# Context norms folded on GpSimd, and two one-vector modulation banks summed on VectorE

## The chip, the cores and the metric

The kernel runs on one core of one Trainium2 chip. What is measured is the device time of one execution, in microseconds (us); several executions are timed, and one more is recorded by the hardware profiler. The engines are named as the profile names them: PE is TensorE (PEld its weight loads), DVE is VectorE, ACT is ScalarE, POOL is GpSimd, SP is the queue that issues nearly all loads. Each engine works through its own instructions in order.

## What is computed

Two transformer blocks in float32 on 256 tokens of width 1024 (`xT` holds them as 128 partitions x 8 chunks x 256 tokens). The first block is attention and a mixture of 32 experts; the second has two layers with a second token stream, the context, that is modulated, mixed and normed like the tokens in its first layer. Cut to what matters here:

```python
# first block: w_ada is 1024 x 6144
mod = silu(c) @ w_ada + b_ada
shift1, scale1, gate1, shift2, scale2, gate2 = split(mod, 6)
h = rms_norm(x, norm1_g) * (1 + scale1) + shift1
x = x + gate1 * (attention(h) @ w_out)
h2 = rms_norm(x, norm2_g) * (1 + scale2) + shift2
x = x + gate2 * moe_ffn(h2)
# second block, layer 0, the context (256 tokens); modc from ada_w and c_ctx
hc = rms_norm(xc, mix_pre_g) * (1 + scc1) + shc1
y = silu(layer_norm(depthwise_conv31(glu(hc @ w_in)), conv_norm_g, conv_norm_b))   # one of three branches
xc = xc + gc1 * rms_norm(merge_of_branches @ w_out, mix_post_g)
hc2 = rms_norm(xc, ffn_pre_g) * (1 + scc2) + shc2
xc = xc + gc2 * rms_norm(square(relu(hc2 @ w_ff1)) @ w_ff2, ffn_post_g)
# then two layers of the second block on x, with keys and values of the context
```

## The kernel before

**Matrix products.** Each weight block of 1024x512 is loaded, split into a high part (ACT, `whi`, L342) and a low part (DVE, `wlo`, L343), and multiplied with activations that are split in the same way: three matmuls for each product, 96 of them for a block (`lin_steps`, L365).

**Two streams.** The main stream is the first block: `front` (attention up to the residual, L687), `route`, `moe`. Beside it goes the *side* stream, `ctx_pass`: the context through the first layer of the second block. It is emitted in steps between steps of the main stream, while `self.side` is true; its tiles end in s (`whis`, `sqs`) and its PSUM tiles are named `side`. The main stream has the higher priority. A scheduler puts the instructions of both streams in one order per engine by its own estimate of times, and the engines then keep this order. When both are done, the *tail* (`self.tail`) runs the two layers of the second block.

**Modulation banks.** A third of a modulation (2048 of 6144 columns) is a *bank*. The side stream computes six of them: "00", "a1", "a2", then "01", "02", "10". The banks a1 and a2 are the second and third of the first block's `w_ada` and serve a single vector, `s1`; the others serve two vectors. `ada_pieces` (L409) loads a bank in eight rows of 128x2048 (1 MB each), into slots of tiles that the side stream does not yet use (`hhi`, `phi`, `hlo`, `plo`), and works off each row with four matmuls that have the 32 padded vectors as weights and stream 512 columns (L438). At the end ACT copies the sum (L443), four transposes bring it to columns (L446), and DVE adds the bias (L451). The front needs a1 for the gate of its residual and a2 for the norm behind it.

**Norms.** `norm_sums` (L245) squares the 8 chunks in four pieces of 128x512, in turn on ACT (L252) and DVE (L254). `stats_add` (L200) adds the squares over the partitions with one matmul of 128x1 for each chunk and half of the tokens, 16 for a norm. `rstd_from` (L163 to L173) makes the reciprocal root with nine small DVE operations (`rs_vs`, `rs_rs`), `bcast_tok` (L179) brings it to all partitions with two transposes. The side stream has five such norms: of the context itself, of the convolution branch, of the mixer's residual, the one ahead of the feed-forward part, and of the last residual.

**The convolution's norm** (`conv_norm`, L1612) has two forms. In the tail, POOL adds the two halves of the chunks (L1617) and folds the sum to one chunk, one matmul against `ones` sums up and spreads it (L1620), and four DVE operations subtract the mean (L1622). On the side, 16 matmuls sum up (L1629), DVE makes the mean (L1632), two transposes spread it (L179) and eight DVE operations subtract it (L1635). The tail's norms use `folded_stats` (L261): the squares are added on POOL (L272) and folded there to one chunk (`fold`, L192), so that `stats_add` works on that chunk alone.

Of the kernel before, what the change touches and what calls it, by code (L numbers as in the profile page):

```python
# [15 lines left out]
OP = mybir.AluOpType  # L16
# [4 lines left out]
P = 128  # L21
D = 1024
KC = 8
GW = 128
T = 256
# [73 lines left out]
class Builder:  # L99
# [158 lines left out]
    def norm_stats(self, xT):  # L258
        return self.stats_end(self.norm_sums(xT), 1.0 / D)
# [149 lines left out]
    def ada_pieces(self, w, b, sT, badd, mod, nv, slots=(), spool=None):  # L409

        nc = self.nc
        acc = []
# [40 lines left out]
        return [lambda k=k: rows(k) for k in range(KC)] + [end]  # L453

# [966 lines left out]
    def ctx_pass(self, L, cx):  # L1421

        nc, a = self.nc, self.a
        w = lambda c: self.wblk("w_in_2", 0, c)
# [3 lines left out]
        ada = {"a": lambda b: self.ada_bank(a["w_ada"][0], b, self.s1, self.colA[:, 16:64], self.mod1, 1, slots),  # L1428
               "0": lambda b: [f() for f in self.layer_ada(0, L, b, slots)],
               "1": lambda b: [f() for f in self.layer_ada(1, self.L1, b, slots)]}  # L1430
        slots = ["hhi", "phi", "hlo", "plo"]
# [9 lines left out]
        slots = ["raws", "phi", "plo"]  # L1441
# [170 lines left out]
    def conv_norm(self, L, yc, chi, clo, pool):  # L1612
        nc = self.nc
        self.pop_conv(1000)
        if self.tail:
            b = self.t(pool, [P, KC, T], tag="qn")[:, 0:4, :]
            nc.gpsimd.tensor_add(b, yc[:, 0:4, :], yc[:, 4:8, :])  # L1617
            self.fold(b)
            mb = self.ps("tr")[:, :T]
            nc.tensor.matmul(mb, self.ones, b[:, 0, :], start=True, stop=True)  # L1620
            for c in range(0, KC, 2):
                nc.vector.scalar_tensor_tensor(yc[:, c:c + 2, :], mb.unsqueeze(1).to_broadcast([P, 2, T]), -1.0 / D,  # L1622
                                               yc[:, c:c + 2, :], op0=OP.mult, op1=OP.add)
            bc = self.folded_stats(yc, self.t(pool, [P, KC, T], tag="qn")[:, 0:4, :])
        else:
            s = self.ps("tr")
            for c in range(KC):
                for t in range(2):
                    nc.tensor.matmul(s[:, t:t + 1], yc[:, c, t * P:(t + 1) * P], self.ones[:, 0:1],  # L1629
                                     start=(c == 0 and t == 0), stop=(c == KC - 1), skip_group_check=True)  # L1630
            mu = self.st([P, 2], tag="mu")
            nc.vector.tensor_scalar(mu, s[:, 0:2], 1.0 / D, None, op0=OP.mult)  # L1632
            mb = self.bcast_tok([mu[:, 0:1], mu[:, 1:2]])
            for c in range(KC):
                nc.vector.tensor_sub(yc[:, c, :], yc[:, c, :], mb)  # L1635
            bc = self.norm_stats(yc)
# [244 lines left out]
```

## Time and profile before

| | us |
|---|---|
| time, median of 3 runs (lowest to highest) | 2755.56 (2747.72 to 2760.62) |
| the profiled execution | 2754.71 |
| its span | 2752.8 |
| stage: first bank of `w_ada` and first norm | 0 to some 40 |
| stage: attention and w_out of the first block (`front`) | to 262 |
| stage: `route` | to some 320 |
| stage: experts, with the context beside them to some 1276 | to some 1590 |
| stage: tail, two layers | to 2753 |

The banks a1 and a2 lie between 96 and 174 us, the context's norms at 174 to 190, 720 to 754, 887 to 910 and 1256 to 1268 us. Busy time of PE is modelled from the starts of its matmuls, and a matmul of float32 leaves two or more records: eight records of L200 are four matmuls. PEclk in the profile is the clock that PE was granted, as a share of 2.4 GHz; 0.50 is the lower level of 1.2 GHz.

### The profile page before, as it was taken

The page shows a single profiled execution, that of the slowest core. Times are in us where ns is not written, and L with a number is a line of the kernel's source. Part 1 is how long each engine was busy: PE and PEld are TensorE (multiplying, and loading weights), DVE is VectorE, ACT ScalarE, POOL GpSimd, SP SyncE. Part 2 cuts the span into 40 slices and gives each one's busy share as a digit, 9 for nine tenths or more (in the row PEclk, how much of TensorE's full clock was granted, in tenths as well). Part 3 has the DMA queues.
Part 4 walks back from the last instruction along what each step waited for, and adds up shares of the span by engine and source line. Part 5 has one row for each costly group of instructions (what it writes and reads, how often), then busy time and mean ns, then how long its engine had stood idle before and what let it go on. Part 6 is the DMA issues. An engine that isn't in the chain of part 4 may idle for free. (4 is left out here: it accounts for less than half of the span.)

```text
span 2752.8 us, 49781 instructions
## 1 busy us (share of the span) xinstructions
PE 2592.5 (94%) x20358; PEld 2047.0 (74%) x20359; DVE 1626.1 (59%) x3090; ACT 1157.5 (42%) x1987; POOL 322.2 (12%) x334
## 2 busy tenths in 40 slices
PE   7999999999899999999889978899999998999998
PEld 5657877678567777875333477899789987899998
DVE  3465543778554524443121279988546789996655
ACT  2333343333243323431111156765445566656543
POOL 0000000000000000000000025442001055350000
PEclk9989899999999999999999989999999999999999
DMA  9758599989999999999999934326854443344442
GB/s 398 300 226 296 203 401 417 364 347 405 378 357 386 390 361 361 409 419 363 392 392 421 415 129 168 125 105 238 289 203 184 158 180 123 131 146 184 154 184 85
DMA packets 119370, 769.80 MB, mean 280 GB/s; under 512 B 11632, under 2 KB 12016, under 8 KB 52832
## 3 DMA queue, kind: packets, MB, share of 16 engines
q1 hardware_dynamic: 117744, 759.15, 70.6%
q0 software_dynamic: 1392, 7.41, 0.7%
q8 instruction: 162, 2.65, 0.4%
q14 instruction: 72, 0.59, 0.1%
HBM read 762.84 MB, written 3.67 MB: 278 GB/s over the span
## 5 line engine op out<-in xcount | busy, mean ns | idle before, releaser
L343 DVE TENSOR_TENSOR wlo<-raw,whi 128x1024 fp32r<-128x1024 f32 (+1 forms) x288 | 337.6, 1175 | 162.2 <-ACT whi L342 156.6
L365 PE MATMUL lin<-hhi,wlo 128*128 128x256 f32 x1440 | 399.3, 283 | 21.6 <-DVE wlo L343 21.6
L365 PE MATMUL lin<-hhi,whi 128*128 128x256 f32 x1440 | 400.5, 282 | 2.2 <-ACT hhi L284 2.2
L365 PE MATMUL lin<-hlo,whi 128*128 128x256 f32 x1440 | 401.4, 281 | 0.1
L342 ACT ACTIVATE whi<-raw 128x1024 fp32r<-128x1024 f32 (+1 forms) x288 | 276.9, 963 | 257.9 <-PE lin L365 189.3
L981 PE MATMUL mlin<-raw,hG 128*32 128x256 f32 (+2 forms) x2920 | 341.3, 456 | 17.5 <-DMA raw<-in_w_gate_up_dram 17.5
L365 PEld LDWEIGHTS lin<-hhi,wlo 128*128 128x128 f32 x1440 | 269.5, 190 | 37.5 <-DVE wlo L343 33.2
L1585 POOL TENSOR_TENSOR yc<-yc,ctmp 128x256 f32<-128x256 f32 x240 | 252.4, 1075 | 300.6 <-ACT ctmp L1584 300.1
L343 DVE TENSOR_TENSOR wlos<-raws,whis 128x512 fp32r<-128x512 f32 x246 | 166.2, 687 | 196.3 <-ACT whis L342 189.4
L365 PEld LDWEIGHTS lin<-hhi,whi 128*128 128x128 f32 x1440 | 271.0, 189 | 5.8 <-ACT hhi L284 3.7
L365 PEld LDWEIGHTS lin<-hlo,whi 128*128 128x128 f32 x1440 | 272.2, 189 | 3.7 <-issue 2.3
L981 PEld LDWEIGHTS mlin<-raw,hG 128*32 128x32 f32 (+2 forms) x2920 | 129.9, 121 | 178.6 <-issue 110.0
L342 ACT ACTIVATE whis<-raws 128x512 fp32r<-128x512 f32 x246 | 148.9, 627 | 225.6 <-PE side L365 186.2
L365 PE MATMUL side<-hhi,whis 128*128 128x256 f32 x720 | 203.0, 288 | 0.1
L365 PE MATMUL side<-hlo,whis 128*128 128x256 f32 x720 | 199.7, 282 | 0.0
L365 PE MATMUL side<-hhi,wlos 128*128 128x256 f32 x720 | 193.1, 284 | 0.7 <-DVE wlos L343 0.5
L343 DVE TENSOR_TENSOR wlo<-raws,whi 128x1024 fp32r<-128x1024 f32 x108 | 139.0, 1287 | 74.4 <-ACT whi L342 73.8
L1587 DVE SCALAR_TENSOR_TENSOR yc<-gl,cw,yc 128x256 f32<-128x256 f32 x240 | 167.8, 734 | 0.1
L342 ACT ACTIVATE whi<-raws 128x1024 fp32r<-128x1024 f32 x108 | 114.4, 1059 | 118.8 <-PE lin L365 103.8
L1006 PE MATMUL main<-raw,aT 128*32 128x256 f32 (+2 forms) x1408 | 162.6, 453 | 1.1 <-DMA raw<-in_w_down_dram 1.0
L365 PEld LDWEIGHTS side<-hhi,whis 128*128 128x128 f32 x720 | 136.7, 190 | 16.5 <-issue 11.2
L365 PE MATMUL lin<-ahi,whi 128*128 128x256 f32 x528 | 145.7, 279 | 0.0
(603 smaller groups left out, 5737.4 us busy)
## 6 DMA issues: line engine op xcount, KB each, us to landing
raw<-in_w_gate_up_dram SPq DMA_DIRECT2D x120, 2048.0 KB, 11.5
raw<-in_w_down_dram SPq DMA_DIRECT2D x55, 2048.0 KB, 11.1
raw<-in_w_in_dram SPq DMA_DIRECT2D x60, 1024.0 KB, 7.1
raws<-in_w_in_dram SPq DMA_DIRECT2D x95, 512.0 KB, 6.8
raws<-in_w_ff_dram SPq DMA_DIRECT2D x88, 512.0 KB, 8.1
raw<-in_w_ff_dram SPq DMA_DIRECT2D x44, 1024.0 KB, 7.0
phi<-in_ada_w_dram SPq DMA_DIRECT2D x10, 1024.0 KB, 7.4
plo<-in_ada_w_dram SPq DMA_DIRECT2D x10, 1024.0 KB, 7.1
```

The lines of the kernel that those rows point to most:

```text
L342: x = nc.scalar.activation(flat(hi), flat(rows[i]), AF.Copy)
L343: y = nc.vector.tensor_sub(flat(lo), flat(rows[i]), flat(hi).bitcast(F32))
L365: x = nc.tensor.matmul(*args, skip_group_check=True, **kw)
L981: nc.tensor.matmul(d, hT(k), gu[k][c0 // D][:, c0 % D:c0 % D + W], start=False, stop=(k == KC - 1), skip_group_check=True)
L1006: nc.tensor.matmul(pys[h][g * C:(g + 1) * C, :W], st, dn[m][:, c0:c0 + W], start=(m == 0), stop=(m == KC - 1), skip_group_check=True)
L1585: nc.gpsimd.tensor_add(d, d, m)
L1587: self.paced(1, nc.vector.scalar_tensor_tensor(d, x, wcol, d, op0=OP.mult, op1=OP.add))
```

## The change

`norm_stats` on the side goes to `folded_stats`: ACT squares four chunks in one operation of 128x1024 and two more in one of 128x512, DVE squares the last two, POOL adds them up in two operations and folds 512 and 256 columns, and two matmuls of 128x1 remain of the 16. `conv_norm` takes the tail's form on the side too. The banks a1 and a2 go through the new `ada_sums`: DVE multiplies each half of a row, 128x1024, by the vector's entry of each partition and adds it to a sum in the tile `plo` (two operations without a second tensor, L466 of the changed kernel, and 14 with one, L468, for a bank); 16 matmuls of 128x1 with the sum as weights and `ones` as the streamed column (L471) add it over the partitions straight into columns, and DVE adds the bias (L473). The rows have three slots there and not four.

```diff
@@ -256,6 +256,8 @@
         return st
 
     def norm_stats(self, xT):
+        if self.side:
+            return self.folded_stats(xT, self.t(self.cx, [P, 4, T], tag="kv"))
         return self.stats_end(self.norm_sums(xT), 1.0 / D)
 
     def folded_stats(self, xT, b):
@@ -451,6 +453,24 @@
                 nc.vector.tensor_add(dst, pv[:, :, :, v], bb)
 
         return [lambda k=k: rows(k) for k in range(KC)] + [end]
+
+    def ada_sums(self, w, b, scol, badd, mod, slots, spool, acc):
+
+        nc = self.nc
+        for k in range(KC):
+            r = self.t(spool, [P, 2048], tag=slots[k % len(slots)])
+            self.behind_first(nc.sync.dma_start(r, w[k * P:(k + 1) * P, b * 2048:(b + 1) * 2048]))
+            for h in range(2):
+                x, d = r[:, h * D:(h + 1) * D], acc[:, h * D:(h + 1) * D]
+                if k == 0:
+                    nc.vector.tensor_scalar(d, x, scol[:, k:k + 1], None, op0=OP.mult)
+                else:
+                    nc.vector.scalar_tensor_tensor(d, x, scol[:, k:k + 1], d, op0=OP.mult, op1=OP.add)
+        p = self.ps("mm")
+        for j in range(16):
+            nc.tensor.matmul(p[:, j:j + 1], acc[:, j * P:(j + 1) * P], self.ones[:, 0:1], start=True, stop=True,
+                             skip_group_check=True)
+        nc.vector.tensor_add(mod[:, b * 16:(b + 1) * 16], p[:, 0:16], badd[:, b * 16:(b + 1) * 16])
 
     def ada_bank(self, *args):
         for f in self.ada_pieces(*args):
@@ -1425,7 +1445,9 @@
         v = 1
         xc = self.t(cx, [P, KC, T], tag="m8")
         self.behind_first(nc.sync.dma_start(xc, a["ctxT"]))
-        ada = {"a": lambda b: self.ada_bank(a["w_ada"][0], b, self.s1, self.colA[:, 16:64], self.mod1, 1, slots),
+        ada = {"a": lambda b: self.ada_sums(a["w_ada"][0], b, self.s1[:, :, 0], self.colA[:, 16:64],
+                                            self.mod1[:, 0, :], ["hhi", "phi", "hlo"], cx,
+                                            self.t(cx, [P, 2048], tag="plo")),
                "0": lambda b: [f() for f in self.layer_ada(0, L, b, slots)],
                "1": lambda b: [f() for f in self.layer_ada(1, self.L1, b, slots)]}
         slots = ["hhi", "phi", "hlo", "plo"]
@@ -1612,28 +1634,16 @@
     def conv_norm(self, L, yc, chi, clo, pool):
         nc = self.nc
         self.pop_conv(1000)
-        if self.tail:
-            b = self.t(pool, [P, KC, T], tag="qn")[:, 0:4, :]
-            nc.gpsimd.tensor_add(b, yc[:, 0:4, :], yc[:, 4:8, :])
-            self.fold(b)
-            mb = self.ps("tr")[:, :T]
-            nc.tensor.matmul(mb, self.ones, b[:, 0, :], start=True, stop=True)
-            for c in range(0, KC, 2):
-                nc.vector.scalar_tensor_tensor(yc[:, c:c + 2, :], mb.unsqueeze(1).to_broadcast([P, 2, T]), -1.0 / D,
-                                               yc[:, c:c + 2, :], op0=OP.mult, op1=OP.add)
-            bc = self.folded_stats(yc, self.t(pool, [P, KC, T], tag="qn")[:, 0:4, :])
-        else:
-            s = self.ps("tr")
-            for c in range(KC):
-                for t in range(2):
-                    nc.tensor.matmul(s[:, t:t + 1], yc[:, c, t * P:(t + 1) * P], self.ones[:, 0:1],
-                                     start=(c == 0 and t == 0), stop=(c == KC - 1), skip_group_check=True)
-            mu = self.st([P, 2], tag="mu")
-            nc.vector.tensor_scalar(mu, s[:, 0:2], 1.0 / D, None, op0=OP.mult)
-            mb = self.bcast_tok([mu[:, 0:1], mu[:, 1:2]])
-            for c in range(KC):
-                nc.vector.tensor_sub(yc[:, c, :], yc[:, c, :], mb)
-            bc = self.norm_stats(yc)
+        four = lambda: self.t(pool, [P, KC, T], tag="qn")[:, 0:4, :] if self.tail else self.t(pool, [P, 4, T], tag="kv")
+        b = four()
+        nc.gpsimd.tensor_add(b, yc[:, 0:4, :], yc[:, 4:8, :])
+        self.fold(b)
+        mb = self.ps("tr")[:, :T]
+        nc.tensor.matmul(mb, self.ones, b[:, 0, :], start=True, stop=True)
+        for c in range(0, KC, 2):
+            nc.vector.scalar_tensor_tensor(yc[:, c:c + 2, :], mb.unsqueeze(1).to_broadcast([P, 2, T]), -1.0 / D,
+                                           yc[:, c:c + 2, :], op0=OP.mult, op1=OP.add)
+        bc = self.folded_stats(yc, four())
         hb = self.st([P, KC], tag="hb")
         nc.vector.tensor_scalar(hb, L["cbn"], 0.5, None, op0=OP.mult)
         for k in range(KC):
```

From `ada_sums` on the line numbers of the changed kernel are 20 higher than before (2 higher between `norm_stats` and there). The order of the program shows the following.

DVE behind the end of the first context bank, before (`modL` is that bank's modulation; `se`, `srd` and `smx` belong to the attention's softmax, `wlo` to a projection's weights):

```order
L451 TENSOR_TENSOR modL_16_101<-side_327,vec_66 128x4x4 x2
L581 SCALAR_TENSOR_TENSOR se_1195,sden_1204<-se_1195,tab_1190 128x128
L461 SCALAR_TENSOR_TENSOR La_71_334<-modL_16_101,vec_66 128x8
L581 SCALAR_TENSOR_TENSOR se_1195,sden_1213<-se_1195,tab_1190 128x256
L461 SCALAR_TENSOR_TENSOR La_72_336<-modL_16_101,vec_66 128x8
L584 RECIPROCAL srd_1207<-sden_1204 128x1
L584 RECIPROCAL srd_1216<-sden_1213 128x1
L617 TENSOR_SCALAR se_1195<-se_1195,srd_1207 128x128
L617 TENSOR_SCALAR se_1195<-se_1195,srd_1216 128x256
L343 TENSOR_TENSOR wlo_1472<-raw_1434,whi_1471 128x512
```

The same place after (`plo` holds the sum of bank a1, `hhi`, `phi` and `hlo` its rows; `sqs` are squares of the context's first norm):

```order
L466 TENSOR_SCALAR plo_338<-hhi_339,s_6_78 128x1024 x2
L345 TENSOR_TENSOR wlo_1448<-raw_1410,whi_1447 128x512
L468 SCALAR_TENSOR_TENSOR plo_338<-phi_343,s_6_78,plo_338 128x1024 x2
L345 TENSOR_TENSOR wlo_1464<-raw_1410,whi_1463 128x512
L271 TENSOR_TENSOR sqs_634<-m_59_274 128x512
L588 SCALAR_TENSOR_TENSOR se_1202<-tab_1166,main_1203 128x384
L468 SCALAR_TENSOR_TENSOR plo_338<-hlo_347,s_6_78,plo_338 128x1024
L345 TENSOR_TENSOR wlo_1480<-raw_1410,whi_1479 128x512
L468 SCALAR_TENSOR_TENSOR plo_338<-hlo_347,s_6_78,plo_338 128x1024
L345 TENSOR_TENSOR wlo_1496<-raw_1410,whi_1495 128x512
```

Sums have come between the weight splits and the softmax; 30 of the 32 stand ahead of the fourth and last `rs_v` (L163, 128x16) of the front's per-head norms, and two right behind it.

PE at the norm of the mixer's residual, before (`raw` are experts' weights, `hG` their tokens, `side_9385` the sums of squares, `side_9422` the spread result):

```order
L981 MATMUL mlin_9110<-raw_9104,hG_8599 32x256 x4
L981 MATMUL mlin_9111<-raw_9104,hG_8599 32x256 x4
L200 MATMUL side_9385<-ones_72,sqs_9398 128x1 x4
L200 MATMUL side_9385<-ones_72,sqs_9404 128x1 x4
L179 MATMUL side_9422<-cst_68,rs_rs_9412 128x128 x2
L981 MATMUL mlin_9110<-raw_1679_9106,hG_8599 32x256 x4
```

and after (`kv` is the folded sum):

```order
L1001 MATMUL mlin_9054<-raw_9050,hG_8543 32x256 x4
L1001 MATMUL mlin_9055<-raw_9050,hG_8543 32x256 x4
L200 MATMUL side_9339<-ones_72,kv_9329 128x1 x2
L179 MATMUL side_9354<-cst_68,rs_rs_9344 128x128 x2
L1001 MATMUL mlin_9054<-raw_1675_9052,hG_8543 32x256 x4
```

Two matmuls with the folded sum stand where the last eight of the 16 were; the others stood among matmuls ahead of this piece, and the next norm's first squares no longer follow right behind. The transposes again stand directly after them. At the next norm, 15 rows further on, the pair stands in the same way, with a row of expert matmuls on either side.

In the order of SP the loads of both streams stand as before, but for a few places. The instructions of the tail stand in the same order on all engines.

## Rows read from the trace of the kernel before

**Rows 1.** The page: busy time of each engine, then slices (tenths, 68.8 us each).

```profile
PE 2592.5 (94%) x20358; PEld 2047.0 (74%) x20359; DVE 1626.1 (59%) x3090; ACT 1157.5 (42%) x1987; POOL 322.2 (12%) x334
...
PE   7999999999899999999889978899999998999998
...
DMA  9758599989999999999999934326854443344442
```

**Rows 2.** Busy time by engine in three stretches of the front.

```profile
core 0: us, PE busy (x) PEld busy (x) DVE busy (x) ACT busy (x) POOL busy (x), PEclk, DMA share, GB/s
96.30:152.80 56.50, 56.50 (x415) 39.74 (x414) 29.11 (x90) 20.68 (x39) 0.00 (x0) 1.00 0.75 287
152.80:200.00 47.20, 44.39 (x228) 24.99 (x227) 28.51 (x103) 16.63 (x35) 0.56 (x1) 0.82 0.42 159
200.00:262.10 62.10, 59.49 (x422) 37.05 (x425) 34.60 (x128) 25.82 (x69) 0.28 (x3) 0.95 0.92 342
```

**Rows 3.** The same view, columns as above, windows of the MoE stretch.

```profile
720.00:740.00 20.00, 18.29 (x150) 13.32 (x152) 7.62 (x22) 4.53 (x10) 0.43 (x1) 0.82 0.76 299
880.00:920.00 40.00, 35.88 (x342) 25.73 (x341) 22.63 (x64) 9.97 (x21) 0.40 (x1) 0.83 0.93 355
1240.00:1280.00 40.00, 39.13 (x284) 25.11 (x283) 21.07 (x51) 8.06 (x15) 0.94 (x2) 0.96 0.86 321
340.00:1580.00 1240.00, 1178.29 (x9409) 796.39 (x9409) 552.25 (x1173) 369.12 (x700) 14.70 (x33) 0.98 0.97 388
```

**Rows 4.** Timeline of PE, 53 to 55 us (start, duration, then line and operation).

```profile
53.57 1.07 PE L438 MATMUL side<-hlo,s 128*32 128x512 f32 x8
54.45 1.04 PE L438 MATMUL side<-plo,s 128*32 128x512 f32 x8
```

**Rows 5.** Timeline of PE, 173 to 190 us.

```profile
172.88 0.60 PE L446 MATMUL side<-cst,sqs 128*128 128x128 f32 x4
174.26 1.05 PE L200 MATMUL side<-ones,sqs 128*128 128x1 f32 x8 [0.78 <-ACT sqs L252]
...
184.45 1.87 PE L200 MATMUL side<-ones,sqs 128*128 128x1 f32 x8
```

**Rows 6.** The page: costliest groups; busy us, mean ns, then idle before.

```profile
L343 DVE TENSOR_TENSOR wlo<-raw,whi 128x1024 fp32r<-128x1024 f32 (+1 forms) x288 | 337.6, 1175 | 162.2 <-ACT whi L342 156.6
...
L343 DVE TENSOR_TENSOR wlos<-raws,whis 128x512 fp32r<-128x512 f32 x246 | 166.2, 687 | 196.3 <-ACT whis L342 189.4
```

**Rows 7.** Instructions of L438, 95.5 to 153 us (min/median/max ns, first, last start).

```profile
L438 PE MATMUL side<-phi,s x24: 592/605/617, 95.8 to 140.7; 128*32 128x512 f32 x24
```

**Rows 8.** Timeline of DVE, 884 to 916 us.

```profile
887.84 1.29 DVE L343 TENSOR_TENSOR wlos<-raws,whis 128x512 fp32r<-128x512 f32 x2 [4.22 <-ACT whis L342]
```

**Rows 9.** Timeline of PE, 718 to 756 us.

```profile
720.21 1.95 PE L1629 MATMUL side<-ones,y 128*128 128x1 f32 x16 [0.63 <-DVE y L1587]
...
754.12 0.28 PE L365 MATMUL side<-hhi,whis 128*128 128x256 f32 x1
754.23 0.28 PE L365 MATMUL side<-hlo,whis 128*128 128x256 f32 x1
```

**Rows 10.** Groups of GpSimd in the tail; columns as in rows 6.

```profile
L192 POOL TENSOR_TENSOR qn<-qn 128x512 f32<-128x512 f32 x4 | 7.8, 1942 | 0.3
L272 POOL TENSOR_TENSOR qn<-qn,sq 128x512 f32<-128x512 f32 x4 | 7.3, 1853 | 17.3 <-DVE sq L269 9.0 <-ACT sq L271 8.3
...
L192 POOL TENSOR_TENSOR qn<-qn 128x256 f32<-128x256 f32 x4 | 6.0, 1489 | 0.3
...
L192 POOL TENSOR_TENSOR sq<-sq 128x256 f32<-128x256 f32 x4 | 3.0, 739 | 0.3
```

**Rows 11.** Timeline of PE, 884 to 916 us.

```profile
887.90 1.05 PE L200 MATMUL side<-ones,sqs 128*128 128x1 f32 x8
889.79 1.05 PE L200 MATMUL side<-ones,sqs 128*128 128x1 f32 x8 [0.84 <-DVE sqs L254]
892.76 0.41 PE L179 MATMUL side<-cst,rs_rs 128*128 128x128 f32 x2 [1.92 <-DVE rs_rs L173]
```

## The prediction

> **What bounds the kernel now.** I began with the page's busy shares and slices [rows 1]: TensorE (PE) is busy 94% of the span and its row reads 8 or 9 nearly everywhere, so work taken off PE could show. The slices also show the DMA row at 9 (once 8) from the sixth to the 23rd slice, where PE is at 7 to 9 too; two resources are nearly full there, and only one of them is relieved. So the limits have to be read stage by stage, and the tail after 1593 us, which the change leaves alone (the program order of its instructions is the same), drops out of the sum.
>
> In the front I read the busy time of each engine over three stretches [rows 2]. They are cut where DVE does something whose place can be found again in the changed program: the end of the first context bank at 96.3 us (`modL`, L451), the fourth and last `rs_v` of the front's per-head norms at 152.8, and the end of the front at 262.1 (the residual, L687). In the first stretch PE is busy for all 56.5 us at full clock and DVE for 29.1: PE is the bound. In the other two PE is idle for 2.8 and 2.6 us, and the granted clock of the middle one is 0.82, so the half level (1.2 of 2.4 GHz) is taken for part of it.
>
> In the MoE stretch the same view, over 340 to 1580 us, gives a DMA share of 0.97, at 388 GB/s, beside 1178 us of PE [rows 3]. DMA is the limit there, except where it pauses: 720 to 740 (0.76), 880 to 920 (0.93) and 1240 to 1280 (0.86). These are the places of the context stream's norms. The idle share of these windows is 4.8, 2.8 and 5.6 us: 13.2 us, and no relief of PE in the MoE stretch can be worth more than that.
>
> **The banks.** A row of a bank is four 32x512 matmuls, eight records, and the next row starts 0.88 us later [rows 4]. Eight rows and the four L446 transposes (0.60 us [rows 5]) are 7.6 us a bank, 15.3 for the two. In their place come 16 matmuls of 128x1 per bank; four such (eight records) take 1.05 us [rows 5], so 4 us a bank. PE gains 7 us.
>
> DVE pays. 32 operations of 128x1024 come in, and the page has a 128x1024 fp32 tensor operation at 1175 ns [rows 6]; at that price they are 37.6 us (the four without a second tensor may be cheaper, which I leave out). By the program order 30 of them stand between the `modL` and the fourth `rs_v`, that is in the first stretch. Its DVE work becomes 29.1 + 30 x 1.175 = 64.4 us, with a square of the context norm (0.7) about 65, against a stretch of 56.5. PE's own need falls there: 12 bank rows go (four slots with 24 records each, one shown in [rows 7], 96 records) at 0.88, 10.6 us, and 0.6 for L446, and 4 come, so about 49. So DVE takes over as the bound, and the stretch is at least 65 long. It waited for PE and ACT for 27 us before; now sums stand in most of these gaps, but in a fixed order, so I add 0.5 to the 8.5: **+9 us**. The ends are +6 and +20: operations of DVE in a row overlap by some 0.08 us (two of 128x512, 687 ns each [rows 6], take 1.29 us together [rows 8]), which makes 1.095 of 1.175; and 11 us of the old waits may remain.
>
> From 152.8 to 262.1 PE gains: the last four rows (3.5), L446 (0.6), and the first context norm. Its 16 matmuls against `ones` ran at half clock for part, the first four in 1.05 us and the last four in 1.87 [rows 5]; the four groups make 6.1 and two waits before them 1.6, of which a pair of matmuls (0.5) stays: 7.2. Against that stand the second bank's 16 small matmuls (4.0). And by the program order 50 projection matmuls of the context now stand in the w_out part, ahead of the end of the front, where none stood before; at 0.115 us from start to start [rows 9] that is 5.8. 11.3 - 4.0 - 5.8 is **-1.5 us**. The 50 matmuls are about half a 512-column block of weights (1 MB of 2 MB), which the MoE stretch then need not load: at 388 GB/s **-2.5 us**.
>
> **The folded norms.** Each loses 14 of 16 small matmuls, 3.5 us of PE at 0.25, and gets a chain on GpSimd (POOL): two adds of 128x512, a fold of 512 and one of 256. POOL adds nothing up for the context before, so the price is read from the tail: 1853, 1942 and 1489 ns, a chain of 7.1 us. Another 128x256 fold of the tail takes 739 ns [rows 10]; with all four at half their price it is 3.6. DVE splits weights beside it here, but does less than in the tail, so I take 5.5, and 1 us for the squares ahead.
>
> *Conv norm* (720 us). The 16 matmuls for the mean (eight of them are the 1.95 us of [rows 9]) become one of 128x256, and the 16 for the squares become two: about 7 us off PE. The POOL add of 128x1024 (some 3 us, by 1.9 for 512 [rows 10]) and two chains take their place, but one DVE pass in four operations replaces eight, and the squares no longer stand behind expert matmuls on PE. I take the whole pause, **-4.8 us**.
>
> *Residual norm and second norm* (886 to 910 us). Before, PE worked off the first norm's last squares from 887.9, waited 0.84 for a square and 1.92 for the `rs_rs` chain of nine small operations, and had the transposes out at 893.2 [rows 11]. In the changed order the two matmuls and the two transposes stand directly one behind the other, and the expert matmuls behind both. PE waits for the POOL chain (6.5 us, less some 2 of expert work in front) and then again for 1.9. So what is saved (3.5 each) is spent: **0**, from -2.8 (the pause of this window goes) to +6 (two waits of 3 us added).
>
> *Last residual norm* (1256 us). Again two matmuls for 16, 3.5 us, in windows with 5.6 us of pause. Nothing of the context stands behind it: **-3.5 us**, from -5.6 to 0.
>
> The Trainium skill ("SBUF — State Buffer", Who interferes with whom) says that a DVE operation with two SBUF inputs and a GpSimd operation that reads SBUF hold a shared port pair exclusively, and the second one is fully blocked; this speaks against putting adds on POOL next to weight splits. The two prices of the 128x256 fold in the tail, 1489 and 739 ns [rows 10], agree with it, but no row before shows such an add beside a weight split of the context. By the rule in full the chains are at the dear end, 1.6 us each, and five of them and the mean's adds move the sum from 2751 to some 2758; by the cheap end it would be some 2745.
>
> **The sum.** The profiled execution took 2754.7 us (span 2752.8), 0.9 below the median of the three runs, 2755.6. 2754.7 + 9 - 1.5 - 2.5 - 4.8 + 0 - 3.5 = **2751 us**, 0.15% below. The measurement cannot tell less than about 0.5% (13.8 us) from no change, so this is "no change". Its own range is 2742 to 2768: the upper end has the first stretch at +20 and a gain of 5 less at the norms.
>
> **Rivals.**
> *All of PE's relief counts.* The sums fit into DVE's 27 idle microseconds of the first stretch without delaying what PE waits for, and DMA closes all its pauses: 7 + 7.2 in the front, 13 in the MoE stretch, 27 us, **2728**. For it: PE is at 100% in the first stretch, DVE at half. Against it: 65 us of DVE work in 56.5. A milder form, the first stretch at +2 with the pauses closed, gives about 2738. Chance of either 0.28.
>
> *DVE becomes the bound and the loss stays*, the rival on the slower side. The mechanism is the DVE queue from 96 to 153 us: a weight split or a softmax step stands behind two sums (2.35 us), PE waits for it, and the last query and key projection arrives late; what follows is a chain through attention and w_out that nothing shortens. The price: the stretch at 75 to 82 us instead of 56.5, +18 to +25, with gains of 4 left elsewhere: **2769 to 2776**. If PE's waits bring the half level of the clock into this stretch, as the middle one shows it, it is dearer: by the 1.87 to 1.05 of [rows 5], a fifth of PE's 49 us at that level adds 8. It decides against my forecast from a distance of about 75 us between `modL` and the fourth `rs_v`. Chance 0.22.
>
> *The POOL chain stalls PE at each of the norms* and the pauses stay: front +5, nothing else, **2760**. Here the change does not do what it is said to do, and it lies within no change.
>
> **How the numbers follow.** Faster by over 0.5% (below 2741.8): 0.28, from the first rival. Within 0.5%: 0.50, of which about 0.15 is the POOL rival. Slower (above 2769.3): 0.22. The range is 2730 to 2774: it leaves out the lower tail of the first rival (a tenth) and the upper end of the second (a tenth).
>
> **What would show it.** In the profile after: DVE busy near 65 us between `modL` and the fourth `rs_v`, and that distance 65 to 70 us with PE idle in it by 10 or more (the first rival: below 60; the second: above 75). The residual L687 at 268 to 272 instead of 262. The two context norms near 890 us with waits of PE side transposes and `ones` matmuls of 3 to 7 us; the DMA share at 720 to 740 above 0.9, and at 1240 to 1280 above 0.9. The tail must have its length of before, 1160 us; if that moves by more than 3 us, the change touches something that I have not seen. Wrong would be above all a cheaper or dearer accumulate operation than 1.175 us, and waits on the three row slots (one less than before) in the front, which would hold the sums back although DVE is free.

## The result

The changed kernel takes 2769.6 us in the median (2763.4 to 2778.8), the kernel before 2753.5 in the runs beside it: a ratio of 1.0066, 95% interval 1.0054 to 1.0079. It is 0.66% slower, some 18 us, where I had forecast no change at 2751 us. The profiled execution of the changed kernel took 2773.35 us with a span of 2771.6, 18.8 more than before.

The first line of the page after answers to [rows 1]: PE lost 17 us of work, DVE and POOL gained 35 each, and the span still grew.

```profile
PE 2575.5 (93%) x20114; PEld 2044.9 (74%) x20115; DVE 1661.5 (60%) x3112; ACT 1159.0 (42%) x1985; POOL 357.3 (13%) x357
```

Busy time by engine after, in windows cut where [rows 2] were cut (`modL`, the fourth `rs_v`, the end of the front, here the start of its last residual operations, 1.1 us ahead of the cut in [rows 2]), then to the first expert matmul, to the tail's first `rs_v`, and the tail (columns: length; busy time of PE, PEld, DVE, ACT, POOL; granted clock; DMA share; GB/s):

```profile
98.10:172.30 74.20, 58.11 (x371) 50.85 (x372) 66.56 (x121) 23.38 (x43) 6.92 (x4) 0.86 0.70 269
172.30:288.20 115.90, 103.55 (x648) 66.38 (x648) 62.74 (x230) 39.40 (x97) 0.79 (x3) 0.81 0.65 233
...
288.20:346.90 58.70, 57.14 (x389) 53.58 (x390) 34.81 (x139) 21.20 (x41) 5.59 (x11) 0.80 0.48 165
346.90:1618.90 1272.00, 1188.76 (x9468) 798.41 (x9467) 564.18 (x1194) 381.68 (x715) 40.40 (x57) 0.97 0.95 383
1618.90:2771.60 1152.70, 1088.67 (x8738) 1020.92 (x8738) 893.13 (x1309) 665.02 (x1037) 300.87 (x269) 0.98 0.45 164
```

The same of before, for the four windows that [rows 2] do not have:

```profile
152.80:261.00 108.20, 102.78 (x640) 61.46 (x640) 62.00 (x228) 41.92 (x101) 0.79 (x3) 0.89 0.70 262
...
261.00:325.90 64.90, 64.26 (x448) 58.67 (x447) 36.00 (x136) 22.91 (x45) 5.20 (x11) 0.82 0.37 131
325.90:1600.30 1274.40, 1202.55 (x9615) 813.78 (x9614) 569.28 (x1216) 379.95 (x717) 16.48 (x38) 0.98 0.96 385
1600.30:2752.80 1152.50, 1088.28 (x8738) 1020.38 (x8738) 890.36 (x1309) 665.41 (x1037) 296.97 (x269) 0.99 0.45 164
```

By stage: 1.8 us ahead of `modL`, +17.7 to the fourth `rs_v`, +7.7 to the end of the front, -6.2 in the route, -2.4 in the MoE stretch, +0.2 in the tail. By the lengths of the stages the loss arises in the front, and nearly a third of it comes back later. The loads tell it a little differently. These are the windows from the start to the first expert matmul, before and then after:

```profile
0.00:325.90 325.90, 301.64 (x2007) 212.83 (x2009) 166.44 (x569) 112.17 (x234) 8.73 (x27) 0.92 0.72 278
```

```profile
0.00:346.90 346.90, 298.10 (x1916) 225.56 (x1920) 204.16 (x611) 112.33 (x233) 16.04 (x31) 0.86 0.71 269
```

The experts start 21 us later, with 93.3 MB moved instead of 90.6. At the 388 GB/s of [rows 3] I estimate these 2.7 MB at 7 us, but the MoE stretch is only 2.4 us shorter: part of the loss arises there too.

**The first stretch** is DVE's. It is busy for 66.6 of 74.2 us (29.1 of 56.5 before), PE for 58. In DVE's timeline one sees the sums in a row with the weight splits:

```profile
98.92 1.41 DVE L466 TENSOR_SCALAR plo<-hhi,s 128x1024 f32<-128x1024 f32 x2
...
100.85 3.48 DVE L468 SCALAR_TENSOR_TENSOR plo<-phi,s,plo 128x1024 f32<-128x1024 f32 x2
...
105.92 2.06 DVE L468 SCALAR_TENSOR_TENSOR plo<-hlo,s,plo 128x1024 f32<-128x1024 f32 x1
107.90 1.74 DVE L345 TENSOR_TENSOR wlo<-raw,whi 128x512 fp32r<-128x512 f32 x1
...
112.97 2.47 DVE L468 SCALAR_TENSOR_TENSOR plo<-hhi,s,plo 128x1024 f32<-128x1024 f32 x2
...
172.32 0.17 DVE L163 TENSOR_SCALAR rs_v<-main 128x16 f32<-128x16 f32 x1 [0.50 <-PE main L557]
```

Two sums take 2.47 us, and the 3.48, 2.06 and 1.74 stand where POOL folds the first context norm. DVE's largest waits in this stretch, with what ended them (us, times, longest), are most of the other 7.6 us:

```profile
DVE y L568 <- PE main L565: 2.6, 1, 2.6
DVE wlo L345 <- ACT whi L344: 2.6, 4, 1.1
DVE se L588 <- PE main L586: 1.1, 1, 1.1
```

PE, which did not stand still here before, waits for 16.1 us:

```profile
PE main L611 <- DVE srd L604: 9.4, 1, 9.4
PE mlin L367 <- DVE wlo L345: 4.3, 3, 3.1
PE mlin L367 <- DVE y L552: 2.4, 1, 2.4
```

The longest wait ends at 166.86 us, when the reciprocal of a softmax (`srd`) is there. In the 9.4 us before that, DVE ran four sums between the steps of this softmax; the last two and the reciprocal are

```profile
162.68 2.47 DVE L468 SCALAR_TENSOR_TENSOR plo<-phi,s,plo 128x1024 f32<-128x1024 f32 x2
...
166.02 0.16 DVE L604 RECIPROCAL srd<-sden 128x1 f32<-128x1 f32 x1
```

The granted clock of this stretch is 0.86, where it was 1.00.

**Behind it** PE waits for rows of the next banks that come late, twice for more than a microsecond (6.4 us of such waits in this window, 1.6 in the same one before):

```profile
221.65 1.94 PE L440 MATMUL side<-phi,s 128*32 128x512 f32 x8 [3.61 <-DMA phi<-in_ada_w_dram]
225.10 1.93 PE L440 MATMUL side<-plo,s 128*32 128x512 f32 x8 [1.51 <-DMA plo<-in_ada_w_dram]
```

The eight records of a row take 1.9 us there, at a granted clock of 0.52 from 220 to 230 us, against 1.07 in [rows 4], where the clock from 50 to 60 us was 1.00.

**In the MoE stretch** the pauses that [rows 3] show did not close (windows moved with the norms; there 0.76, 0.93 and 0.86):

```profile
740.00:760.00 20.00, 18.84 (x136) 10.46 (x136) 8.32 (x19) 4.43 (x9) 7.30 (x7) 0.85 0.76 298
900.00:940.00 40.00, 27.49 (x241) 17.38 (x241) 21.55 (x60) 11.39 (x24) 9.84 (x9) 0.70 0.79 308
1260.00:1300.00 40.00, 34.01 (x216) 18.88 (x216) 18.53 (x45) 6.58 (x12) 5.49 (x6) 0.83 0.83 319
```

The middle one is worse by 0.14. PE's timeline answers to [rows 11]: where a square cost it 0.84, the folded sum costs 5.31, and the chain behind it 1.92 as before.

```profile
909.30 1.01 PE L200 MATMUL side<-ones,kv 128*128 128x1 f32 x4 [5.31 <-POOL kv L192]
...
912.23 0.66 PE L179 MATMUL side<-cst,rs_rs 128*128 128x128 f32 x2 [1.92 <-DVE rs_rs L173]
```

### The profile page after: what moved, and what is told of

Same layout as the page of the kernel before. It is cut to its first block, busy times and chain, and to the rows that moved or that the text cites. A ratio compares the mean times of both kernels' runs of the same rounds, so it can differ in the third digit from the quotient of the medians.

```text
span 2771.6 us, 49339 instructions
## 1 busy us (share of the span) xinstructions
PE 2575.5 (93%) x20114; PEld 2044.9 (74%) x20115; DVE 1661.5 (60%) x3112; ACT 1159.0 (42%) x1985; POOL 357.3 (13%) x357
```

## The experiments

My theory was that DVE's queue in the first stretch makes the loss; the rivals were the folds on POOL, and later the row slots. Each kernel ran in five rounds beside the kernel before (E4 in three). "Idle" is the time that DMA did nothing from the start to the tail's first `rs_v`, summed over windows of 10 us as (1 - DMA share) x length (a share above 1 counts as 1), in the one profiled execution. All kernels move the same 580 MB by then, so this is bookkeeping of where the time went, not a cause. The tail has its old length after the change, but over the experiments it is 1149 to 1164 us long for the same work, and a profiled execution lies up to 10 us from the median of its kernel, so a few us between two profiles show nothing. The ratios come from all executions; the difference of two ratios in the table is uncertain by some 6 to 10 us.

| kernel | banks on DVE | row slots | context norms | ratio (95%) | us by it | idle |
|---|---|---|---|---|---|---|
| before | none | 4 | matmuls | 1 | 0 | 156 |
| the change | a1, a2 | 3 | POOL | 1.0066 (1.0054 to 1.0079) | +18 | 179 |
| E1 | a1, a2 | 3 | matmuls | 1.0066 (1.0043 to 1.0090) | +18 | 167 |
| E2 | none | 4 | POOL | 1.0042 (1.0021 to 1.0063) | +12 | 163 |
| E3 | a1 | 3 | POOL | 0.9967 (0.9951 to 0.9984) | -9 | 139 |
| E4 | a1, a2, half | 3 | POOL | 1.0008 (0.9991 to 1.0026) | +2 | 153 |
| E5 | a1 | 3 | matmuls | 1.0010 (0.9993 to 1.0028) | +3 | 153 |
| E6 | none | 4 | POOL, conv only | 1.0037 (1.0021 to 1.0053) | +10 | 159 |
| E7 | none | 4 | DVE | 0.9993 (0.9977 to 1.0009) | -2 | 151 |
| E8 | a1 | 3 | DVE | 0.9987 (0.9970 to 1.0004) | -4 | 144 |
| E9 | a2 | 3 | POOL | 1.0019 (1.0000 to 1.0038) | +5 | 155 |
| E10 | a1, a2 | 4 | POOL | 0.9998 (0.9977 to 1.0019) | -1 | 153 |
| E11 | none | 4 | POOL, longer | 1.0075 (1.0047 to 1.0102) | +21 | 174 |
| E12 | a1, a2 | 3 | DVE | 1.0049 (1.0028 to 1.0070) | +13 | 164 |
| E13 | a1, a2 | 4 | matmuls | 1.0060 (1.0037 to 1.0083) | +17 | 170 |
| E14 | a1, a2 | 4 | DVE | 0.9970 (0.9952 to 0.9987) | -8 | 146 |
| E15 | none | 3 | matmuls | 1.0039 (1.0021 to 1.0057) | +11 | 167 |
| E16 | a1 | 4 | POOL | 0.9971 (0.9955 to 0.9987) | -8 | 137 |
| E17 | a1, a2 | 4 | first on POOL | 1.0014 (1.0000 to 1.0028) | +4 | 160 |
| E18 | a1 | 4 | DVE | 0.9998 (0.9981 to 1.0016) | -1 | 148 |

### The parts alone

**E1** undoes the norms, **E2** the banks:

```diff
     def norm_stats(self, xT):
-        if self.side:
-            return self.folded_stats(xT, self.t(self.cx, [P, 4, T], tag="kv"))
...
-        ada = {"a": lambda b: self.ada_sums(
+        ada = {"a": lambda b: self.ada_bank(
```

> Only the banks a1 and a2 are summed on DVE; all norms of the context are as before. Theory (DVE queue): the 32 sums of 1.27 us fill DVE between modL and the fourth rs_v, that stretch is 72 to 76 us long and not 56.5, the front ends 24 to 30 us later than before, and the time is 18 to 26 us above before, more than the whole change (+16), since the norms' gain is missing. Rival (POOL folds): the loss comes from the folds on GpSimd, which wait for DVE and hold PE; then this kernel is within 5 us of before.

> Only the norms of the context are folded on GpSimd and its convolution norm takes the tail's form; the banks a1 and a2 go through PE as before. Theory (DVE queue): the front is as before or up to 5 us shorter (first context norm), the MoE stretch gains 2 to 5 us, the time is 2 to 9 us below before. Rival (POOL folds): 10 to 20 us above before, with waits of PE side L200 and L179 of several us at 890 to 910.

E1 went as the theory had it in the stretch (74.1 us) and in the time. Its front ended 18 us later, not 24 to 30, and its profiled execution, the fastest of its six, only 8.6 us later than that of before: as in the changed kernel, part of the front's delay came back. E2 went as the rival had it, 12 us slower where I expected a gain: PE waits 14.3 us for folded sums between 700 and 960 us, and the DMA share falls behind these waits. But the two do not add up: +18 and +12 make +18 together.

E2, waits of PE from 700 to 960 us (columns as above), and its busy times around the two norms:

```profile
PE side L200 <- POOL kv L192: 14.3, 3, 5.8
```

```profile
880.00:920.00 40.00, 25.82 (x240) 17.32 (x238) 21.83 (x61) 8.72 (x17) 10.31 (x9) 0.74 0.77 303
```

### How much of the sums, and where

**E3** sums a1 alone, **E9** a2 alone (with 2 for 1), **E5** is E3 with the old norms; **E4** leaves operations out:

```diff
-        ada = {"a": lambda b: self.ada_sums(
+        ada = {"a": lambda b: (self.ada_sums(
...
+) if b == 1 else self.ada_bank(a["w_ada"][0], b, self.s1, self.colA[:, 16:64], self.mod1, 1, slots),
```

```diff
-                else:
+                elif h == 0:
                     nc.vector.scalar_tensor_tensor(d, x, scol[:, k:k + 1], d, op0=OP.mult, op1=OP.add)
```

> The whole change, but only bank a1 is summed on DVE; a2 goes through PE as before. 16 of the 32 sums, all ahead of the third rs_v. Theory (DVE queue): only the part from modL to the third rs_v is full, it is 33 to 34 us as in the changed kernel (27.4 before), the next part to the fourth rs_v is 29 to 31 us as before, the front ends 5 to 10 us later, the time is between 3 us below and 6 us above before. Rival (proportional: the loss is what slots and late rows cost per bank): half of the loss of both banks, 8 to 13 us above before.

> The whole change, but in both banks only the first half of each row behind the first is added up: 14 of the 32 operations are left out, so two thirds of the modulation's columns of these banks are not the reference's. Loads, slots and matmuls stay. Theory (DVE queue): the stretch from modL to the fourth rs_v needs 18 us less of DVE and is 56 to 61 us long, the front ends 0 to 8 us later than before, the time is between 4 us below and 5 us above before. Rival (slots and loads: three slots and their release order hold the rows of 01 and 02 back): the stretch stays above 66 us and the time 10 to 18 us above before.

> The kernel before with one edit: bank a1 alone is summed on DVE; a2 through PE, all context norms as before. The run with this and the folded norms was 11 us below the kernel before, the folded norms alone 10 above it. Theory (two separate costs, the banks in the front, the folds in the MoE stretch): PE's waits for the folds are gone, the route brings in 12 MB or more as in that run, the time is 16 to 26 us below before. Rival (the gain comes from the two together, by where the scheduler then puts the loads): between 8 us below and 8 us above before.

> The whole change, but only bank a2 is summed on DVE and a1 goes through PE as before; the program order puts 3 of its 16 sums ahead of the fourth rs_v and the rest behind. Theory (DVE queue between modL and the fourth rs_v): that stretch is 56 to 60 us as before, the front ends 0 to 6 us later than before, and the time is that of the folded norms (10 above before) or less: 0 to 10 us above. Rival (it is the number of banks on DVE, wherever they stand): the stretch is some 62 us as with a1 alone, and the time is 11 us below before, as there.

E4's stretch is 51.7 us with DVE at 43.8, E3's 62.4 with 47.4:

```profile
98.40:150.10 51.70, 47.39 (x345) 42.66 (x346) 43.79 (x102) 20.13 (x37) 6.93 (x4) 0.93 0.70 265
```

```profile
97.90:160.30 62.40, 56.86 (x395) 46.49 (x396) 47.37 (x105) 21.95 (x40) 0.00 (x0) 0.95 0.74 279
```

With all 32 sums DVE is busiest in this stretch and it is long (66.6 of 74.2 us); with 16 or 18 of them PE is busiest again (56.9 of 62.4, 47.4 of 51.7), and the long wait for the softmax is gone. In E9, with nearly all sums behind the stretch, it is 58.2. E4 is the cleanest test: with slots, loads and norms as they are, 14 sums fewer take 16 of the 18 us away. So the loss of the change needs DVE's work, which also holds the row slots. The time does not follow the stretch in the same way: E3, 6 us longer there than before, is 9 us faster in all, with the front's end at the old place, which neither expectation had; E5, with a like stretch (63.9) and the old norms, is 3 us slower. My expectation for E5, that the two costs are separate, fell. E9 fits its theory but for a front that ended 9 us later.

### The folds

**E7**, **E8** and **E12** make the same adds on DVE for the context (the first cut shows one of three such places); **E6** folds the convolution's norm alone; **E11** lengthens the chain by four adds in each norm (second cut):

```diff
-            self.nc.gpsimd.tensor_add(x[:, 0:n, :], x[:, 0:n, :], x[:, n:2 * n, :])
+            (self.nc.vector if self.side else self.nc.gpsimd).tensor_add(x[:, 0:n, :], x[:, 0:n, :], x[:, n:2 * n, :])
```

```diff
-            nc.gpsimd.tensor_add(b[:, 2 * j:2 * j + 2, :], b[:, 2 * j:2 * j + 2, :], sq)
+            for _ in range(3 if self.side else 1):
+                nc.gpsimd.tensor_add(b[:, 2 * j:2 * j + 2, :], b[:, 2 * j:2 * j + 2, :], sq)
```

> The kernel before with one edit: the convolution's norm of the context in the tail's form (its mean and its squares folded on GpSimd), the four other context norms by 16 matmuls, the banks as before. Theory (a fold costs where PE stands still behind it): the wait at 740 us stays, the two at 890 to 910 and the one at 1265 go, the time is 0 to 5 us above before. Rival (the convolution norm is where the folds gain, the others lose): 3 to 8 us below before.

> The folded norms without the summed banks (10 us above before), with the same adds and folds on DVE instead of GpSimd, for the context only. A chain is then some 2.5 to 3 us instead of 5.5 to 6. Theory (PE stands behind the chain, so its length counts): PE's waits for the folded sum fall from 14 us to 3 to 7 between 700 and 960 us, the time is between 4 us below and 4 us above before. Rival (not the chain but the new order of PE and loads costs): still 7 to 12 us above before, with shorter waits.

> Bank a1 alone summed on DVE and all context norms folded on DVE. Theory (two separate costs): the sum of the two kernels with one of these each, that is 15 to 25 us below before, and below the one with folds on GpSimd (11 below). Rival (DVE, already the busiest beside PE, cannot take the folds too): 0 to 10 us below before.

> The folded norms without the summed banks (10 us above before), with each of the two adds of a norm's squares done three times, so that the norms of the context are not the reference's: a chain on GpSimd is 5 us longer. Theory (PE stands behind the chain, experts' loads stop behind PE): PE's waits for the folded sum grow by 8 to 20 us over the MoE stretch, the time is 16 to 26 us above before. Rival (the chain's length does not matter, the order of PE and loads does): 5 to 13 us above before.

> The whole change (16 us above before) with the context's folds on DVE and not on GpSimd. Theory (two costs that add up, the front's DVE queue and the folds): the front ends some 27 us later as in the changed kernel, DMA's pauses in the MoE stretch are 5 to 12 us less than there, the time is 2 to 10 us above before. Rival (the loss of the whole change is the front's alone): 13 to 20 us above before.

With the banks left alone the time goes up with the chain: on DVE -2 us, on POOL +12, POOL with four more adds +21. The step from E7 to E2 is clear of the noise and has its wait: PE's waits for the sum from 700 to 960 us are 3.3 and 14.3, and the DMA share around the two norms 1.01 and 0.77. The step to E11 is just within the uncertainty, and E11's waits are 16.4 us, only 2 more where I expected 8 to 20, at a share of 0.78; what made it slower is not shown. E7 and then E11:

```profile
PE side L200 <- DVE kv L192: 3.3, 2, 2.7
```

```profile
870.00:915.00 45.00, 37.91 (x348) 23.52 (x347) 30.83 (x81) 15.29 (x31) 2.10 (x2) 0.92 1.01 412
```

```profile
PE side L200 <- POOL kv L192: 16.4, 3, 12.5
```

```profile
895.00:945.00 50.00, 28.33 (x298) 19.14 (x291) 26.66 (x66) 10.76 (x22) 19.69 (x16) 0.76 0.78 301
```

Beside the summed banks the sign changes from pair to pair: DVE instead of POOL gives -5 (the change to E12), -8 (E10 to E14), +6 (E3 to E8) and +7 us (E16 to E18); the first and the third are within the uncertainty. E8 came out as its rival had it, E12 in the time as its rival, with a front that ended 16 us later and not 27. In E3 the waits are as long (12.0 us at the two norms) and the share there is 0.96; in E10 they are 13.3 us, at no loss. PE stands still just as much, but DMA goes on. Why the order that the scheduler makes gives such moments in one kernel and not in another stays open. So does E6, which neither expectation had: slower by 10 with one norm folded, though PE waits only 1.2 us for a folded sum from 700 to 960 us.

### The slots

**E10** gives the summed banks the fourth slot back, **E15** takes it from the kernel before, which sums on PE:

```diff
-                                            self.mod1[:, 0, :], ["hhi", "phi", "hlo"], cx,
-                                            self.t(cx, [P, 2048], tag="plo")),
+                                            self.mod1[:, 0, :], ["hhi", "phi", "hlo", "plo"], cx,
+                                            [self.t(cx, [P, 4, T], tag="g4").rearrange("p c t -> p (c t)"),
+                                             self.t(cx, [P, 1024], tag="rawx")]),
...
-self.ada_bank(a["w_ada"][0], b, self.s1, self.colA[:, 16:64], self.mod1, 1, slots),
+self.ada_bank(a["w_ada"][0], b, self.s1, self.colA[:, 16:64], self.mod1, 1, slots[:3]),
```

> The whole change with four row slots for the summed banks as before, not three: the sums go to two other free tiles. Theory (DVE's work is the bound): the stretch stays above 70 us, PE idles in it for more than 10, the time is 10 to 22 us above before. Rival (the rows have too few slots, and SP's queue waits for DVE to free them): the stretch is below 66 us, the time 0 to 8 us above before.

> The kernel before with one edit: the rows of a1 and a2 go through three slots, not four; everything is still summed on PE. Theory (slots cost only because DVE holds them long): within 5 us of before. Rival (the fourth slot is worth its loads by itself): 8 to 18 us above before, with DMA's share between 96 and 174 us lower.

Both expectations for E10 were half right: DVE's stretch is longer still, 84 us, and the front ends 16 us later than before, and yet the time is that of before, 19 us less than with three slots. E15 is the counterpart: its stretch is 55 us, its front ends 2 us earlier than before, and it is 11 us slower; the rival held. E10 and E15, first stretch (and the rest of the front for E15):

```profile
97.50:181.40 83.90, 68.63 (x437) 56.23 (x439) 76.23 (x152) 28.02 (x53) 5.25 (x4) 0.84 0.75 281
```

```profile
98.30:153.40 55.10, 55.10 (x402) 40.33 (x401) 29.60 (x92) 21.60 (x41) 0.00 (x0) 1.00 0.67 251
153.40:258.70 105.30, 100.00 (x603) 60.75 (x603) 58.41 (x224) 39.10 (x96) 0.79 (x3) 0.87 0.62 232
```

DMA's share of E15 is 0.67 and 0.62 where it was 0.75 and 0.70: the missing slot holds loads back. By the first expert matmul, at 320.4 us, they are made up for, 89.7 MB against 90.6 at 325.9; what E15 loses shows between 960 and 1320 us, before and in E15:

```profile
960.00:1320.00 360.00, 351.12 (x2943) 252.78 (x2943) 139.94 (x262) 107.45 (x196) 3.82 (x9) 1.00 0.96 384
```

```profile
960.00:1320.00 360.00, 355.19 (x2993) 262.40 (x2991) 146.91 (x272) 114.81 (x208) 3.83 (x9) 1.00 0.92 363
```

What is late then is the context, not the front. A mark for it is the `rs_vs` of the gated branch (`gsss`), before, after, in E10 and in E15:

```profile
545.13 0.15 DVE L163 TENSOR_SCALAR rs_vs<-gsss 128x2 f32<-128x2 f32 x1
```

```profile
561.50 0.17 DVE L163 TENSOR_SCALAR rs_vs<-gsss 128x2 f32<-128x2 f32 x1
```

```profile
532.80 0.15 DVE L163 TENSOR_SCALAR rs_vs<-gsss 128x2 f32<-128x2 f32 x1
```

```profile
570.52 0.17 DVE L163 TENSOR_SCALAR rs_vs<-gsss 128x2 f32<-128x2 f32 x1
```

The mark does not order the other kernels, though: in E16, 8 us faster than before, it stands at 563.3, and in E2, 12 us slower, at 540.3. That a late context is the cause is not shown.

The rest tries the slot in other company: **E13** the banks with four slots and the old norms, **E17** the same with the first context norm folded, **E14** E10 with folds on DVE, **E16** and **E18** a1 alone with four slots, folds on POOL and on DVE. E17's edit:

```diff
-        self.norm_mod(xc, L["a1", v], L["b1", v], hi, lo)
+        self.norm_mod(xc, L["a1", v], L["b1", v], hi, lo, self.folded_stats(xc, self.t(cx, [P, 4, T], tag="kv")))
```

> The two banks summed on DVE through four row slots, all norms of the context as before. With three slots this was 17 us above before. Theory (three slots that DVE frees late keep the loads waiting, and loads not made in the front are paid for in the MoE stretch): 4 us below to 5 us above before, with less DMA idle ahead of the first expert matmul than with three. Rival (the fourth slot helped only together with the folded norms): 9 to 18 us above before.

> The whole change with four row slots (same as before) and the context's folds on DVE. Theory (the folds on GpSimd hold PE and with it the experts' loads, whatever the banks do): 4 to 14 us below before. Rival (with the banks summed, where the folds run makes no difference, as in the pair with three slots): within 4 us of before.

> Folded norms on GpSimd, bank a1 alone summed on DVE, through four slots; with three it was 11 us below before. Theory (loads earlier, DVE not full): 11 to 20 us below before. Rival (with 16 sums three slots are enough, the fourth changes nothing or takes tiles that are wanted later): 4 to 12 us below before.

> The two banks summed on DVE through four slots, and of the context's norms only the first, in the front, folded on GpSimd; the four in the MoE stretch by 16 matmuls as before. The front's order on DVE is that of the whole change with four slots (0 us), where the same kernel without this fold was 16 us above before. Theory (the first norm's place decides how early the rows of 01 and 02 come; the folds in the MoE stretch cost): first expert matmul at 334 to 338 us, context as far ahead as with the whole change and four slots, the time 5 to 14 us below before. Rival (the folds in the MoE stretch are needed to gain): 5 to 18 us above before.

> The best of each: a1 alone summed on DVE through four slots, all folds of the context on DVE. With folds on GpSimd it was 7 to 8 us below before. Theory (folds on GpSimd hold PE): 10 to 20 us below before. Rival (with bank a1 on DVE the fold's engine does not matter, as with three slots): 4 to 10 us below before.

E13 shows that the slot alone is not enough (+17, where the same kernel with three slots, E1, has +18). E17, which has the order of DVE in the front from E10, is at +4: the first context norm's early place is worth 13 of these 17 us, and the folds in the MoE stretch cost nothing there, since E10, which has them, is not slower. E14 came out as its theory had it and E16 as its rival. E17 and E18 met neither expectation: the best of each is not the best. E3, E14 and E16 are 0.3% faster than the kernel before and beat both kernels; they cannot be told apart.

## Why the prediction was wrong

**What bounds the kernel.** The limits by stage were read rightly: PE in the front, DMA with pauses in the MoE stretch, a tail that keeps its length (1152.5 and 1152.7 us). Two terms of the sum were too small (the waits of the first stretch, and the loads behind it, at nothing), and the gain at the folded norms was not there. A further error is in how I joined them: I took the end of the front as the path and let its delay run through to the end. E10 (front 16 us later, no loss) and E15 (front 2 us earlier, 11 us lost) show that it is not. What has been loaded by the first expert matmul counts as well: E10 starts the experts 10 us later than before, but with 4 MB more moved, which at 388 GB/s I estimate at 11 us. For E15 this account fails, as its loss comes after 960 us. (Of the slices, the DMA row from the sixth to the 23rd reads 8 twice, not once; nothing hangs on it.)

**The banks, first stretch (+9 forecast, +17.7 measured).** The work was sized well, 65 us against 66.6: a sum costs 1.27 and not 1.175, one without a second tensor 0.75, and beside POOL the three places shown took 2.9 us more in all. The step that failed is "so I add 0.5" for the waits in a fixed order: they were 7.6 us, a quarter of those before. On PE's side this is 16 us of standing still, and PE was busy for 58.1 us instead of the 49 that I had counted, at a granted clock of 0.86. It lies within the end that I gave (+20).

**From 152.8 us to the end of the front (-1.5 forecast, +7.7 measured).** The step that failed is "11.3 - 4.0 - 5.8", a sum of matmuls alone. PE's busy time did not fall (103.6 us, 102.8 before), as its clock went from 0.89 to 0.81, and its idle time went from 5.4 to 12.4 us, 4.8 of them waits for rows of the next banks. I counted matmuls and not loads. The diff says "three slots" and I named the slots only among the things that could go wrong. What that line costs depends on the company: 11 us with the sums on PE (E15; 6 to 16 by its interval), 19 in the whole change (against E10), nothing that can be measured with the sums and the old norms (E1 against E13) or with a1 alone (E3 against E16).

**The context's lead (-2.5 forecast).** The sign held: the route is 6.2 us shorter, with 9.7 MB moved in 58.7 us against 8.5 in 64.9.

**The folded norms (-8.3 forecast, -2.4 for the whole MoE stretch).** For the norms at 886 to 910 I had written that PE waits for the chain and then again for 1.9; 5.31 and 1.92 came, and the window lost 0.14 of DMA's share instead of nothing. I took 0 with an end of +6. For the convolution's norm I took the whole pause; its share stayed at 0.76. E2 says what the norms do by themselves: +12, where my terms make -8.3 and some us in the front. PE time saved is not the currency there. In E2 it is PE standing still while the loads stop; E3 and E10 show that the wait alone, without the stop of the loads, need not cost.

**The rivals.** The slower one, the DVE queue, came nearest: it asked for a stretch of 75 to 82 us (74.2) and 2769 to 2776 us (2769.6), at a chance of 0.22. Its mechanism is in the trace, a softmax step behind sums and PE waiting for it. It did not have what followed: 7.7 us more to the end of the front, and 6 given back by the route. The POOL rival was right in its mechanism and would have been 12 us, not 5, in E2. "All of PE's relief counts" is excluded by E1 and E2 both.

**Still open.** That the change loses nothing to speak of when 14 of its 32 sums are left out (E4) or when it has a fourth slot (E10) is shown. The parts do not add up (E1 and E2 against the change; E3 against E2 and E5), and every edit makes the scheduler move loads and norms elsewhere. I can say for each kernel where DMA stood idle, not why one order is kinder. That slots and first norm belong together (E10, E13, E17) is shown; by which load is not.

## What to carry to other kernels

Before moving work to an idle engine, count what its buffers hold back: a tile that becomes an accumulator is a load slot less, and where a later stage is bound by DMA, a slot less can be paid for there (E15: 11 us, though its front was shorter). Read the neighbourhood's waits, not the engine's share of busy time: an engine at half load took 37 us more work in a stretch of 56 and kept 7 us of waits. And where an engine works in order, a short operation that waits 5 us for a chain elsewhere holds all that is queued behind it. Shortening the chain was worth 13 us with the old banks (E2 to E7) and not in every company (E3 to E8, E16 to E18), and with the short chain the 14 matmuls that each norm saves left nothing to measure.

## What the runs showed of the hardware

A fused multiply and add of 128x1024 in fp32 with two tensors took 1.27 us, the multiply alone 0.75. Beside POOL's adds of the first context norm, two of the sums took 3.48 us and not 2.47, a weight split 1.74 and not 0.68, and POOL's own add 2.46 and not 1.28:

```profile
99.60 2.46 POOL L274 TENSOR_TENSOR kv<-kv,sqs 128x512 f32<-128x512 f32 x1 [95.80 <-ACT sqs L273]
105.61 1.28 POOL L274 TENSOR_TENSOR kv<-kv,sqs 128x512 f32<-128x512 f32 x1 [3.56 <-DVE sqs L271]
```

The Trainium skill ("SBUF — State Buffer", Who interferes with whom) says that of two such operations one blocks the other; the trace agrees, with delays of 0.8 to 1.2 us on either side, about the length of one operation of the other. Away from DVE's full queue a whole chain on POOL was 5.5 to 6.0 us in the MoE stretch of E2, near the 5.5 that I took.
